# Moving the matmul operands of a two-block transformer kernel onto multiples of 256 bytes in SBUF

## The chip, the cores and the metric

The kernel runs on one core of a Trainium2 chip. The metric is the device time of one execution in microseconds (us). Three executions of the kernel before took 2682.97, 2686.71 and 2687.61 us; the median is 2686.71 us.

## The reference, cut to what matters

The input `x` is 512 tokens of 1024 features, in fp32. It passes two blocks.

```
first_block, for l in (0, 1):
    h = rms_norm(x); proj = h @ w_in            # 1024 -> 10 pieces
    6 heads of difference attention, 6 heads of grouped attention, 4 heads over a memory of 256
    x = x + rms_norm(concat(heads * silu(gates)) @ w_out)
second_block, for i in (0, 1):
    x = x + 0.5 * rmsnorm(swiglu(rmsnorm(x)))   # 1024 -> 2 x 2816 -> 1024
    x = x + rmsnorm(mixer(rmsnorm(x)))          # i = 0: S5 state space; i = 1: gated convolution, 31 taps
    x = x + 0.5 * rmsnorm(swiglu(rmsnorm(x)))
```

All arithmetic keeps about fp32's precision.

## The kernel before, in words

**Three products for one.** Weights and activations are each split into a high part of the type fp32r (fp32 bits, which TensorE takes in one pass) and a low part, the rest. `mm3` (lines 157 to 161) then issues three matmuls into the same PSUM bank: high by high (L159), high by low (L160), low by high (L161). Nearly every matmul of the kernel comes from these three lines. `load` (lines 134 to 155) brings 128 x 1024 weights per DMA, splits them on ScalarE (L148) and on VectorE or GpSimd (L153), and hands them on by pieces.

**The order of the work.** Eight phases run one after the other: attention layer 0, attention layer 1 (`attn`, lines 351 to 785), the first feed-forward block f00, S5 (`s5`, 1026 to 1157), f01, f10, the convolution (`conv`, 1166 to 1280) and f11. Each ends in an output projection (`out_proj`, 261 to 278, or the tail of `ffn`), which adds to `x` and normalizes the tokens for the next phase. The framework works out the order of instructions on each engine and the places of the tiles; tiles that don't live at the same time share places.

**A feed-forward block** (`ffn`, lines 281 to 348) has 22 hidden blocks of 128. Up, per block: 2 halves x 8 slices of 128 features x 3 matmuls of 512 columns, 48 in all; the stationary operand is a weight slice, the moving one (read column by column) is `self.act(k)`, the normalized activations. The first two blocks are done in two halves of 256 columns (192 matmuls). Down: two passes (keys `DN`, h = 0 and 1), in each 22 slices x 4 tokens blocks x 3 matmuls of 512 columns, 264 in all; the stationary operand is a piece of the gated tile `gts[k]`, the moving one is weights. A gated tile comes from one of two tags:

```
if f not in (4, 5) and f < 12:
    gt = self.tl("u4", [P, 2, 512], F32R)
else:
    if f % 2 == 0:
        pair = self.tl("u8", [P, 2, 2, 512], F32R)
    gt = pair[:, f % 2]
```

The down passes go through k = 0 to 21 in order, and there the tag of the stationary operand is the only thing of the operands that changes (in f00, f01 and f10).

**Where tiles lie.** The framework packs tiles by size from the bottom of SBUF, a partition's 229,376 bytes up to its last 32. In the built program of the kernel before the places of the tiles are these (bytes in a partition, and the remainder to 256):

| tiles | first byte | remainder |
|---|---|---|
| `base`: the activations `act0`, `act1` (line 76), `identr`, `wh` | 16,512 | 128 |
| `x`, then the tag `u8` (among them gated tiles of f = 4, 5 and 12 to 21, queries and keys of the attention, `zz` of the convolution) | 50,784 to 116,320 | 96 |
| `const`: `ident`, `fold`, `ones`, `par` | 116,320 | 96 |
| tags `u4`, `raw`, `w`, `wf` (weights) and smaller ones | 121,088 upward | 0 |

Slices inside these tiles that a matmul reads begin at further multiples of 512 bytes, except `zz[:, p, i:i + 512]` in the convolution's taps (line 1229), which begins 4 bytes later at each tap i. In f11, when `base` is no longer needed, some weight tiles of its down passes are put into that memory and so also have the remainder 128.

**Small things that the change touches.** `mh` holds -0.5 in one column; `pow_` (line 181) reads it on GpSimd as the exponent. It is a column of `const`.

Of the kernel before, what the change touches and what calls it, by code (L numbers as in the profile page):

```python
# [8 lines left out]
F32 = mybir.dt.float32  # L9
F32R = mybir.dt.float32r  # L10
# [4 lines left out]
P = 128  # L15
# [50 lines left out]
class Kern:  # L66
    def __init__(self, ctx, tc, aps):
        self.tc, self.nc, self.a = tc, tc.nc, aps
        nc = self.nc
        self.pool = ctx.enter_context(tc.tile_pool(name="sb", bufs=1))  # L70
        self.psp = ctx.enter_context(tc.tile_pool(name="ps", bufs=1, space=bass.MemoryType.PSUM))
        self.dram = ctx.enter_context(tc.tile_pool(name="dr", bufs=1, space=bass.MemoryType.DRAM))
        self.cnt = 0
        base = self.sb([P, 8568], F32R, "base", 1)
        acts = base[:, 0:8192].rearrange("p (a k r c) -> p a k r c", a=2, k=4, r=2)
        self.act0, self.act1 = acts[:, 0], acts[:, 1]
        self.identr = base[:, 8192:8320]
        rest = self.sb([P, 1192], F32, "const", 1)
        self.par = rest[:, 400:1192]
        self.ident, self.fold, self.mh = rest[:, 0:128], rest[:, 128:192], rest[:, 192:193]  # L80
        self.neglam, self.lam, self.mag, self.s5d, self.bgl = rest[:, 194:196], rest[:, 196:200], rest[:, 200:232], rest[:, 232:264], rest[:, 264:272]
        self.ones = rest[:, 272:400]
        self.wh = base[:, 8320:8568].rearrange("p (f e) -> p f e", f=8)
        make_identity(nc, self.ident)
        nc.vector.tensor_copy(self.identr, self.ident)
        nc.gpsimd.memset(self.mh, -0.5)
        nc.vector.tensor_tensor(out=self.fold, in0=self.ident[:, 0:64], in1=self.ident[:, 64:128], op=ALU.add)
        self.flip = self.turn = self.wcnt = 0
        self.on_pool, self.on_dve = (), ()
        self.wt = "w"  # L90
        self.first = 0
# [1370 lines left out]
```

## Time and profile before

| | |
|---|---|
| median of three executions | 2686.71 us |
| the profiled execution, its own time | 2685.91 us |
| its span, first to last instruction | 2684.1 us |
| PE busy (TensorE matmul) | 95% of the span, 13437 records |
| PEld busy (TensorE weight load) | 81% |
| DVE, ACT, POOL busy | 55%, 39%, 25% |
| mean granted TensorE clock | 0.98 |
| moved by DMA | 98 GB/s on the mean |

DVE is VectorE, ACT ScalarE, POOL GpSimd. A matmul's record lasts longer than the distance to the next one's start, because matmuls are pipelined: records overlap. What a matmul costs in a dense stretch is therefore the stretch divided by the number of matmuls that start in it. The profile names every on-chip tile `t`, so operands are told apart by the line and by the order of the loops.

### The profile page before, as it was taken

The page shows a single profiled execution, that of the slowest core. Times are in us where ns is not written, and L with a number is a line of the kernel's source. Part 1 is how long each engine was busy: PE and PEld are TensorE (multiplying, and loading weights), DVE is VectorE, ACT ScalarE, POOL GpSimd, SP SyncE. Part 2 cuts the span into 40 slices and gives each one's busy share as a digit, 9 for nine tenths or more (in the row PEclk, how much of TensorE's full clock was granted, in tenths as well). Part 3 has the DMA queues.
Part 4 walks back from the last instruction along what each step waited for, and adds up shares of the span by engine and source line. Part 5 has one row for each costly group of instructions (what it writes and reads, how often), then busy time and mean ns, then how long its engine had stood idle before and what let it go on. Part 6 is the DMA issues. An engine that isn't in the chain of part 4 may idle for free.

```text
span 2684.1 us, 34384 instructions
## 1 busy us (share of the span) xinstructions
PE 2558.3 (95%) x13437; PEld 2170.8 (81%) x13437; DVE 1471.3 (55%) x2330; ACT 1034.2 (39%) x1961; POOL 666.4 (25%) x880
## 2 busy tenths in 40 slices
PE   7998999989999999989999999999999966999998
PEld 7997889878888888888888888888888844888887
DVE  7788577875589832595533323433324697533322
ACT  4567554675434432323422223322223423322221
POOL 4653245432256600322200001100003940200000
PEclk9999999999999999989999999999999988999999
DMA  4211232112235433352222222322232210222221
GB/s 150 74 63 66 74 115 74 54 53 73 104 118 188 183 135 121 145 209 75 99 94 91 94 102 87 110 94 94 95 108 77 77 54 25 94 94 102 87 95 71
DMA packets 68898, 262.80 MB, mean 98 GB/s; under 512 B 7936, under 2 KB 8448, under 8 KB 64384
## 3 DMA queue, kind: packets, MB, share of 16 engines
q1 hardware_dynamic: 68736, 260.61, 27.5%
q8 instruction: 105, 1.72, 0.3%
q14 instruction: 57, 0.47, 0.1%
HBM read 239.61 MB, written 20.97 MB: 97 GB/s over the span
## 4 chain that ended last, share of the span: by engine, by line
PE 51%; DVE 3%; POOL 1%; ACT 1%; issue 0%; DVEq 0%; POOLq 0%; ACTq 0%
PE t L160 17%; PE t L161 17%; PE t L159 17%; DVE t L1235 2%; POOL t L153 0%; PE t L1244 0%; PE t L214 0%; PE t L1261 0%; DVE t L1242 0%; ACT t L200 0%; ACT t L148 0%; ACT t L232 0%; PE t L1102 0%; DVE t L206 0%; PE t L1103 0%
## 5 line engine op out<-in xcount | busy, mean ns | idle before, releaser
L159 PE MATMUL t<-t,t 128*128 128x512 f32 (+3 forms) x3571 | 1309.5, 369 | 15.2 <-ACT t L166 12.3
L160 PE MATMUL t<-t,t 128*128 128x512 f32 (+3 forms) x3571 | 1308.8, 367 | 6.8 <-DVE t L167 3.3
L161 PE MATMUL t<-t,t 128*128 128x512 f32 (+3 forms) x3571 | 1304.5, 367 | 2.5 <-DVE t L167 2.4
L159 PEld LDWEIGHTS t<-t,t 128*128 128x128 f32 x3571 | 674.4, 189 | 133.8 <-ACT t L166 17.4
L153 DVE TENSOR_TENSOR t<-t,t 128x1024 fp32r<-128x1024 f32 (+2 forms) x314 | 389.8, 1244 | 706.1 <-ACT t L148 510.8
L160 PEld LDWEIGHTS t<-t,t 128*128 128x128 f32 x3571 | 675.7, 189 | 123.1 <-DVE t L167 6.0
L161 PEld LDWEIGHTS t<-t,t 128*128 128x128 f32 x3571 | 675.4, 189 | 115.1 <-DVE t L167 4.2
L148 ACT ACTIVATE t<-t 128x1024 fp32r<-128x1024 f32 (+2 forms) x370 | 384.0, 1045 | 549.4 <-PE t L160 405.9
L235 POOL TENSOR_SCALAR t<-t,t 128x1 f32<-128x1 f32 x32 | 10.7, 335 | 1322.9 <-ACT t L232 1321.6
L166 ACT ACTIVATE t<-t 128x512 fp32r<-128x512 f32 (+3 forms) x316 | 155.6, 517 | 289.2 <-DVE t L297 119.6
L167 DVE TENSOR_TENSOR t<-t,t 128x512 fp32r<-128x512 f32 (+3 forms) x316 | 198.9, 647 | 75.4 <-ACT t L166 75.2
L153 POOL TENSOR_TENSOR t<-t,t 128x512 fp32r<-128x512 f32 (+4 forms) x102 | 191.0, 1889 | 78.8 <-ACT t L148 56.8
L296 ACT ACTIVATE t<-t 128x512 f32<-128x512 f32 x88 | 52.6, 598 | 308.6 <-PE t L161 296.2
L555 ACT ACTIVATE t<-t,t 128x512 f32<-128x512 f32 (+1 forms) x176 | 113.5, 654 | 39.9 <-DVE t L553 37.5
L1235 DVE SCALAR_TENSOR_TENSOR t<-t,t,t 128x512 f32<-128x512 f32 x161 | 116.3, 752 | 10.9 <-PE t L161 7.5
L553 DVE TENSOR_REDUCE t<-t 128x1 f32<-128x512 f32 (+1 forms) x160 | 105.5, 680 | 16.5 <-PE t L563 7.8
L297 DVE TENSOR_TENSOR t<-t,t 128x512 f32<-128x512 f32 x88 | 60.5, 687 | 84.5 <-PE t L161 84.2
L621 DVE TENSOR_TENSOR t<-t,t 128x512 fp32r<-128x512 f32 x112 | 76.0, 685 | 37.7 <-ACT t L616 31.2
L958 POOL TENSOR_TENSOR t<-t,t 128x64 f32<-128x64 f32 (+3 forms) x112 | 65.8, 606 | 70.5 <-DVE t L886 48.7
L976 DVE TENSOR_TENSOR t<-t,t 128x256 f32<-128x256 f32 x128 | 65.5, 575 | 21.7 <-DMA t<-in_s5bc 21.5
L183 POOL TENSOR_TENSOR t<-t,t 128x1 f32<-128x1 f32 (+2 forms) x98 | 74.1, 757 | 6.9
L206 DVE SCALAR_TENSOR_TENSOR t<-t,t,t 128x512 f32<-128x512 f32 x72 | 57.9, 845 | 26.9 <-POOL t L183 26.9
(220 smaller groups left out, 2165.3 us busy)
## 6 DMA issues: line engine op xcount, KB each, us to landing
t<-in_W SPq DMA_DIRECT2D x356, 512.0 KB, 3.5
mats<-t SPq DMA_DIRECT2D x16, 1024.0 KB, 4.1
t<-mats SPq DMA_DIRECT2D x16, 1024.0 KB, 5.4
t<-in_gv SPq DMA_DIRECT2D x19, 512.0 KB, 3.7
t<-in_W SPq DMA_DIRECT2D x24, 384.0 KB, 3.1
t<-in_W SPq DMA_DIRECT2D x8, 480.0 KB, 4.1
t<-in_x SPq DMA_DIRECT2D x4, 512.0 KB, 7.0
t<-in_mem SPq DMA_DIRECT2D x4, 512.0 KB, 6.2
```

The source lines that it names most:

```text
L148: nc.scalar.activation(h[:, :c], raw[:, :c], AF.Copy)
L153: eng.tensor_tensor(out=l[:, o:o + m], in0=raw[:, o:o + m], in1=h[:, o:o + m].bitcast(F32), op=ALU.subtract)
L159: mm(out, lhs[0], rhs[0], start=start, stop=False)
L160: mm(out, lhs[0], rhs[1], start=False, stop=False)
L161: mm(out, lhs[1], rhs[0], start=False, stop=stop)
L166: nc.scalar.activation(h, src, AF.Copy)
L167: nc.vector.tensor_tensor(out=l, in0=src, in1=h.bitcast(F32), op=ALU.subtract)
L183: self.nc.gpsimd.tensor_tensor(out=r, in0=r, in1=self.mh.to_broadcast([P, n]), op=ALU.pow)
L553: v.tensor_reduce(out=mx[:, q * w:q * w + w], in_=part, axis=AX.X, op=ALU.max, negate=True)
L555: act.activation(e[:, i], part[:, i - q * w], AF.Exp, bias=mx[:, i:i + 1], accum_out=u["d"][:, i:i + 1])
L621: v.tensor_tensor(out=lo, in0=tp, in1=h.bitcast(F32), op=ALU.subtract)
L1235: v.scalar_tensor_tensor(out=pc, in0=z[:, i:i + 512], scalar=cp[:, f, 5 + i:6 + i], in1=pc, op0=ALU.mult, op1=ALU.add)
```

## The change

`base` gets 40 more columns of 4 bytes: 32 in front, which shift everything else in it by 128 bytes, and 8 behind. `mh` moves into the first of the columns in front. `const` gets 24 more columns. Together that is 256 bytes more per partition. No instruction is added or taken away. Packed in the same order, `base` then ends at byte 50,944, `const` begins at 116,480 and the rest at 121,344, all multiples of 256; the activations begin at 16,640, which is one too. `zz` is read at the same 4-byte steps as before.

```
-        base = self.sb([P, 8568], F32R, "base", 1)
+
+        base = self.sb([P, 8608], F32R, "base", 1)
+        self.mh = base[:, 0:1].bitcast(F32)
+        base = base[:, 32:8608]
         acts = base[:, 0:8192].rearrange("p (a k r c) -> p a k r c", a=2, k=4, r=2)
         self.act0, self.act1 = acts[:, 0], acts[:, 1]
         self.identr = base[:, 8192:8320]
-        rest = self.sb([P, 1192], F32, "const", 1)
+        rest = self.sb([P, 1216], F32, "const", 1)
         self.par = rest[:, 400:1192]
-        self.ident, self.fold, self.mh = rest[:, 0:128], rest[:, 128:192], rest[:, 192:193]
+        self.ident, self.fold = rest[:, 0:128], rest[:, 128:192]
```

## Rows read from the trace of the kernel before

**Rows 1.** The page, part 1: busy time, share of the span, instructions.
```profile
PE 2558.3 (95%) x13437; PEld 2170.8 (81%) x13437; DVE 1471.3 (55%) x2330; ACT 1034.2 (39%) x1961; POOL 666.4 (25%) x880
```

**Rows 2.** Busy time by stretch: length; PE, PEld, DVE, ACT, POOL; clock; DMA.
```profile
0.00:303.00 303.00, 274.27 (x1919) 256.37 (x1919) 227.72 (x445) 186.18 (x449) 140.80 (x207) 0.99 0.25 84
303.00:368.00 65.00, 64.23 (x326) 54.24 (x325) 39.58 (x53) 25.58 (x56) 16.98 (x23) 1.00 0.37 130
368.00:648.00 280.00, 260.65 (x1852) 243.67 (x1851) 217.10 (x395) 173.77 (x422) 126.76 (x182) 0.98 0.19 63
...
697.00:1098.00 401.00, 396.60 (x1895) 329.78 (x1896) 252.67 (x565) 144.00 (x255) 133.75 (x227) 0.99 0.39 140
1098.00:1302.00 204.00, 191.35 (x1190) 171.40 (x1190) 143.13 (x158) 71.12 (x139) 57.97 (x57) 0.95 0.37 136
1302.00:1690.00 388.00, 384.21 (x1801) 316.13 (x1800) 137.38 (x149) 116.19 (x165) 28.80 (x35) 1.00 0.28 98
1690.00:2054.00 364.00, 363.33 (x1633) 296.12 (x1631) 120.50 (x130) 103.70 (x139) 10.95 (x16) 1.00 0.27 94
2054.00:2302.00 248.00, 201.70 (x906) 159.16 (x907) 188.36 (x276) 91.55 (x165) 120.43 (x100) 0.90 0.15 54
2302.00:2685.00 383.00, 373.36 (x1702) 304.52 (x1700) 125.78 (x139) 102.44 (x138) 14.35 (x21) 0.99 0.27 94
```

**Rows 3.** PE by stretch, f10's first down pass: k 0-3, 4-5, 6-11, 12-21.
```profile
1929.73:1940.63 10.90, 10.90 (x49) 1.00 0.34 122
1940.63:1946.24 5.61, 5.61 (x25) 1.00 0.35 137
1946.24:1962.59 16.35, 16.35 (x73) 1.00 0.29 97
1962.59:1990.70 28.11, 28.11 (x121) 1.00 0.28 94
```

**Rows 4.** The same: f10's up blocks 2-21; f11's first down pass, k 6-9, 10-11.
```profile
1705.73:1929.73 224.00, 224.00 (x962) 1.00 0.27 94
...
2571.01:2581.92 10.91, 10.91 (x50) 1.00 0.04 15
2581.92:2587.51 5.59, 5.59 (x26) 1.00 0.01 3
```

**Rows 5.** PE in order of time (start, length, line): tap 4, two convolution blocks.
```profile
2097.16 0.39 PE L159 MATMUL t<-t,t 128*128 128x512 f32 x1
2097.38 0.40 PE L160 MATMUL t<-t,t 128*128 128x512 f32 x1
2097.62 0.40 PE L161 MATMUL t<-t,t 128*128 128x512 f32 x1
```

**Rows 6.** The same tap, the convolution's next block of 128 features.
```profile
2111.80 0.39 PE L159 MATMUL t<-t,t 128*128 128x512 f32 x1
2112.02 0.40 PE L160 MATMUL t<-t,t 128*128 128x512 f32 x1
2112.26 0.40 PE L161 MATMUL t<-t,t 128*128 128x512 f32 x1
```

**Rows 7.** PE by stretch, matmuls of one width: 384, 320, 256 columns.
```profile
354.75:360.03 5.28, 5.28 (x32) 1.00 0.88 300
438.29:442.56 4.27, 4.27 (x31) 1.00 0.25 77
1694.94:1705.62 10.68, 10.68 (x92) 1.00 0.27 98
```

**Rows 8.** Waits of PE, 0 to 303 us: us in total, times, longest.
```profile
PE t L214 <- DVE t L206: 11.7, 3, 7.8
```

**Rows 9.** Waits of PE in the convolution, 2054 to 2303 us.
```profile
PE t L1244 <- DVE t L1242: 42.0, 5, 10.0
```

**Rows 10.** The page, parts 5 and 6: the split on ScalarE; the weights' DMAs.
```profile
L148 ACT ACTIVATE t<-t 128x1024 fp32r<-128x1024 f32 (+2 forms) x370 | 384.0, 1045 | 549.4 <-PE t L160 405.9
...
t<-in_W SPq DMA_DIRECT2D x356, 512.0 KB, 3.5
```

## The prediction

> **What bounds the kernel now.** I read the page's busy shares first. PE is busy 95% of the span and no other engine more than 55% apart from its own weight loads [rows 1]. A share over the whole span hides that stages differ, so I cut the span into the phases [rows 2]. There the reader should look for stretches where PE busy equals the length. In the four feed-forward blocks (697 to 1098, 1302 to 1690, 1690 to 2054, 2302 to 2685) PE is busy 1517.5 of 1536 us, at a granted clock of 0.99 to 1.00; DVE is at a third to two thirds and the DMA engines at 0.27 to 0.39 of their time. The first attention layer's output projection (303 to 368) looks the same. In these stretches the time is the number of matmuls times the distance between their starts, and nothing else. The attention's middles (0 to 303 and 368 to 648) have PE busy 534.9 of 583 us; there PE waits for VectorE and ScalarE, the longest sum being for L206, three waits with 11.7 us, 7.8 the longest [rows 8]. The convolution is PE-free for a fifth of its time, and one wait, L1244 for VectorE's L1242, makes up 42.0 us of that [rows 9].
>
> So the question is whether the distance between matmuls depends on where their operands begin. The trace before answers it in one place, because the down passes change the place of the stationary tile in mid-loop and nothing else. In f10 [rows 3] the record counts include one matmul that began before the stretch, so the counts by the loops are 48, 24, 72 and 120. That makes 10.90 / 48 = 227.1 ns for k = 0 to 3, 5.61 / 24 = 233.8 ns for k = 4, 5, then 16.35 / 72 = 227.1 ns, then 28.11 / 120 = 234.3 ns. The quick ones are just those k whose gated tile has the remainder 0, with weights of remainder 0; the slow ones have 96. In f11 k = 6 to 9 take 10.91 / 48 = 227.3 ns, but k = 10, 11, whose gated tiles are still at remainder 0, take 5.59 / 24 = 232.9 ns: there the weights have moved into memory with remainder 128 [rows 4]. The up blocks, moving operand at 128, take 224.00 / 960 = 233.3 ns [rows 4]. One operand off is enough, and a second off costs no more.
>
> **The change, part by part.** The first part is what it does to a matmul of 512 columns: 233.3 - 227.1 = 6.2 ns saved in an up block, 7.0 ns (234.1 on the mean of the slow down rows) in a down pass, 6.5 ns where I have no row of its own (the projections, scores, gates of S5).
>
> The second part is narrower matmuls. No quick row exists for them. The slow rows are 5.28 / 30 = 176 ns for 384 columns, 4.27 / 29 = 147 ns for 320 and 10.68 / 90 = 118.7 ns for 256 [rows 7]. If the loss grows with the columns, a 256-column matmul saves 3.3 ns (half of 6.6); if it is one price per matmul, 6.6 ns. The nearest row doesn't decide, so I take the middle: 5.0 ns for 256, 5.3 for 320, 5.8 for 384, and keep both ends. Nothing excludes that they gain nothing, which the wide range below includes.
>
> The sum, at the profiled execution's 2685.9 us (its span of 2684.1 and 1.8 around it):
> - Feed-forward, PE-bound, so all of it counts. Up: 4 x 960 x 6.2 ns = 23.8 us. First two blocks in halves: 4 x 192 x 5.0 = 3.8 us. Down: 528 matmuls a block, of which 240 are quick already; 288 x 7.0 = 2.0 us in each of f00, f01, f10. In f11, 408 are slow, but some 256 of them read weights in the memory that `base` leaves; that memory still begins at 16,512, remainder 128, so I leave them slow: 152 x 7.0 = 1.1 us. Together 35 us.
> - Attention's output projections, dense in rows 2: 2 x 192 x 6.5 = 2.5 us.
> - Attention's middles. 576 matmuls of 384 columns (3.3 us), 384 of 320 (2.0), 1472 of 256 (gates, memory queries, values, memory scores: 7.4), 288 of 512 (scores, memory projection: 1.9): 14.6 us if PE alone sets the pace, 0 if VectorE and ScalarE do. PE is busy 92% here and VectorE 76% (227.7 + 217.1 of 583 us) [rows 2], so both set the pace by turns; I take half, 7.3 us.
> - S5: its glu and output projection, 2 x 192 x 6.5 = 2.5 us; its input projection 384 x 5.0 = 1.9 us, half of it because it alternates with the scan: 3.5 us.
> - Convolution. The first double projection runs ahead of VectorE: 192 x 5.0 = 1.0 us; the output projection 192 x 6.5 = 1.3 us. The other projections (288 x 6.6 = 1.9 us) run while PE is waiting for VectorE anyway; I cost them at nothing, because that wait of 42.0 us covers it. The taps stay at their 4-byte steps: nothing. Together 2.3 us.
> - The fp32 transposes and the few fp32 products with `ident`, `fold`, `ones`: some 1,700 records of about 110 ns. Bounded by 0 and by the same 2.9%, 5 us; I take 0, since the only quick rows are fp32r.
> - The move of `mh`: GpSimd's powers read another column; no instruction and no wait is added, and writes into other columns of `base` already run beside reads of it, as the dense up blocks after each normalization show. I cost it at nothing; if each power waited half a microsecond, all but those at the ends of phases would still fall beside PE's work.
>
> 35 + 2.5 + 7.3 + 3.5 + 2.3 = 50.6 us, so 2685.9 - 50.6 = 2635.3 us for the profiled execution. The median of the runs stands 0.8 us above that one: 2636 us.
>
> What is late next: in the feed-forward blocks nothing comes near. Per up block PE will need 21.8 us instead of 22.4, and the DMA share would rise from 0.27 to 0.28 [rows 2]. In the attention the waits for VectorE grow; that is the half I left out.
>
> A page bears on the size. The Trainium skill, "TensorE: Matmul & The Clock Gate", section "Wait — 56ns, not 53.3ns?", gives 215.7 ns for 512 columns back to back on a warm array. By that figure, as an estimate from the page, aligned matmuls would save 17.6 ns and not 6.2, and the up blocks alone 68 us. The rows at remainder 0 stand at 227.1 [rows 3], so the trace disagrees and I go by it.
>
> **The rivals.**
> *No change: the place isn't what makes the down rows differ.* In the map, remainder 0 goes together with high memory (from 121,088 up), remainders 96 and 128 with low memory. If TensorE reads high memory quicker, or if only steps smaller than these tiles' remainders matter, nothing gains: 2686 us, within a microsecond. For it: rows 3 and 4 can't tell place from remainder. Against it: the taps. Their two moving operands lie in one low tile, 2,168 bytes apart, and at tap 4 the high part's matmul takes 2097.38 - 2097.16 = 0.22 us and the low part's 0.24 us; in the next block, whose tile lies 4,352 bytes (17 x 256) further, again 0.22 and 0.24 us [rows 5, 6]. The low bits of the address matter inside one region.
> By the Trainium skill, "SBUF — State Buffer", section "Door 1: The DMA port swizzle", SBUF has lines of 16 bytes and only the crossing to a new line costs. Both 96 and 128 are multiples of 16, so by that rule this rival would hold. The steps in rows 3 are not explained by it.
>
> *Partly: only the up blocks or only the stationary operand gain.* After the change the activations lie at an odd multiple of 256 and the weights, 256 bytes further up, at an even one; all quick rows of now have both at odd multiples. If part of the pairs stay slow, between a quarter and two thirds of the sum come: 2653 to 2674 us, say 2660.
>
> *Slower: the new packing makes PE wait for weights in the attention.* SBUF is full to the last 32 bytes, and 256 more are asked for; the packer must hand some places on in another order, and a tile that takes over a place waits for its last reader. The place is the loads of the attention's chunks: 24 of them (12 per layer). One that starts late exposes at least the DMA's landing and the first split, 3.5 and 1.0 us [rows 10]. At 24 x 3 us = 72 us against the gain of 51 us the time is 2707 us; it decides from 2.1 us per chunk. For it: the number of buffers a tag may use is fixed, but not the places. Against it: the tile sizes grow only in the two tiles that live throughout, and PE has few long waits in the attention [rows 8], with the DMA at 0.19 to 0.25.
>
> **How the numbers follow.** The forecast has 0.72, its own range 2613 to 2647. The quick end counts every sum whole (50.6 + 7.3 + 1.0 + 1.9 = 60.8 us, 2626), and takes off 5.5 us for narrow matmuls at 6.6 ns, 5 for fp32 and 1.7 for f11's weights. The slow end counts only feed-forward, with 3.3 ns for narrow matmuls (33.4 us), and the dense projections (6.3 us). Partly has 0.13, no change 0.10, slower 0.05. The range for 8 in 10 is 2609 to 2663: the forecast and the nearer half of the partial case. A change below 0.2%, 5.4 us, can't be told from none here. Faster: 0.72 + 0.13 = 0.85, same 0.10, slower 0.05.
>
> **What would show it.** In the profile after, the up blocks of f10 should take 20 x 48 x 227 ns = 217.9 us where they took 224.0, and the down passes 227 ns from k = 0 to 21 without a step. A 256-column stretch shows whether the narrow price is 3.3 or 6.6. The taps' 0.22 and 0.24 should remain. The granted clock and the wait L1244 for L1242 should stay, the latter perhaps a little longer. The prediction is wrong if up blocks stay at 233 ns (place, not remainder), if they gain and the attention's stretches grow (packing), or if the clock falls below 0.98.

## The result, and the profile after

The changed kernel takes 2656.24 us (median of four executions, 2653.88 to 2657.20) against 2687.03 us before. The ratio is 0.9887 with a 95% interval of 0.9870 to 0.9904. The forecast was 2636 us. The direction holds and so does the wide range (2609 to 2663), but the gain is 30.8 us and not 51, and the time lies outside the range that the forecast itself had (2613 to 2647), inside that of the rival "partly" (2653 to 2674).

The page of the kernel after, part 1, answers to [rows 1]: PE's share is still 95%, with 33 us less of it; the other engines do the same work in nearly the same time.

```profile
PE 2525.2 (95%) x13437; PEld 2175.8 (82%) x13437; DVE 1472.7 (55%) x2330; ACT 1032.8 (39%) x1961; POOL 666.0 (25%) x880
```

Next the dense stretches of f10 after the change, PE by stretch, in the order of rows 4 and 3: the up blocks 2 to 21, then the first down pass with k = 0-3, 4-5, 6-11, 12-21; the last two are f11's k = 6-9 and 10-11.

```profile
1692.07:1909.70 217.63, 217.63 (x963) 1.00 0.28 97
1909.70:1920.58 10.88, 10.88 (x50) 1.00 0.33 119
1920.58:1926.02 5.44, 5.44 (x26) 1.00 0.41 147
1926.02:1942.34 16.32, 16.32 (x74) 1.00 0.27 97
1942.34:1969.54 27.20, 27.20 (x122) 1.00 0.28 97
...
2543.36:2554.24 10.88, 10.88 (x50) 1.00 0.28 96
2554.24:2559.68 5.44, 5.44 (x26) 1.00 0.30 97
```

The up blocks take 217.63 / 960 = 226.7 ns a matmul where they took 233.3 [rows 4]. The down pass has lost its step: 10.88 / 48, 5.44 / 24, 16.32 / 72 and 27.20 / 120 are all 226.7 ns, where k = 4, 5 and 12 to 21 stood at 234 [rows 3]. In f11, k = 10, 11 came down too: in the built program of the kernel after none of that block's weights lie where `base` was any more. Those of k = 10, 11 lie among the other weights, and 64 of the block's matmuls read theirs where `const` was, all at remainder 0.

The narrow matmuls are another matter. These are the stretches that answer to [rows 7]: 384, 320 and 256 columns.

```profile
356.09:361.30 5.21, 5.21 (x31) 1.00 0.91 314
439.60:443.85 4.25, 4.25 (x31) 1.00 0.25 77
1681.16:1691.95 10.79, 10.79 (x91) 1.00 0.27 97
```

384 columns went from 176 to 5.21 / 30 = 173.7 ns, 320 from 147.2 to 146.6, and 256 from 118.7 up to 10.79 / 90 = 119.9 ns.

By phase (the columns of rows 2; the stretches are cut at the phases of the kernel after):

```profile
0.00:304.40 304.40, 275.49 (x1911) 257.28 (x1912) 227.98 (x445) 185.76 (x448) 139.79 (x206) 0.98 0.25 83
...
368.00:647.00 279.00, 260.76 (x1857) 243.31 (x1856) 218.09 (x398) 173.35 (x421) 126.36 (x182) 0.99 0.19 63
...
696.00:1091.00 395.00, 389.52 (x1895) 329.38 (x1896) 254.14 (x565) 143.39 (x255) 133.60 (x227) 0.99 0.39 142
1091.00:1295.00 204.00, 190.37 (x1195) 172.57 (x1193) 142.98 (x158) 70.73 (x139) 58.30 (x57) 0.95 0.38 137
1295.00:1675.00 380.00, 375.35 (x1786) 315.94 (x1785) 137.27 (x149) 115.92 (x164) 29.09 (x34) 1.00 0.29 100
1675.00:2032.00 357.00, 356.07 (x1643) 297.27 (x1641) 121.14 (x130) 104.31 (x142) 11.08 (x16) 1.00 0.27 96
2032.00:2280.00 248.00, 201.59 (x909) 160.95 (x909) 188.46 (x276) 91.48 (x165) 120.39 (x100) 0.89 0.16 54
2280.00:2654.00 374.00, 364.88 (x1697) 305.65 (x1696) 125.40 (x139) 102.24 (x138) 14.10 (x20) 0.99 0.27 96
```

The four feed-forward blocks shrank (401 to 395, 388 to 380, 364 to 357, 383 to 374 us against [rows 2]). The attention's middles (303 and 280 us before), S5 (204) and the convolution (248) did not. The convolution's wait kept its size, as the prediction said of it [rows 9]:

```profile
PE t L1247 <- DVE t L1245: 42.2, 5, 10.0
```

Both kernels issue the same 13437 matmul records in the same order, so the distance from each to the next can be compared one by one between the two traces. I call a pair dense when the clock is full in both and neither distance is over 1.35 times the usual one for its width. Summed over the pairs, before to after: dense 512 columns -41.1 us, 256 columns +2.1, 384 -0.6, 320 -0.1, fp32 and transposes +0.2; pairs at half clock in one of the traces +5.4; pairs with a wait +3.7. The sum is -30.4 us, the difference of the two spans (2684.1 and 2653.8).

### The profile page after: what moved, and what is told of

The parts are those of the page before. It is cut to its first block, busy times and chain, and to the rows that moved or that the text cites. A ratio compares the mean times of both kernels' runs of the same rounds, so it can differ in the third digit from the quotient of the medians.

```text
span 2653.8 us, 34395 instructions
## 1 busy us (share of the span) xinstructions
PE 2525.2 (95%) x13437; PEld 2175.8 (82%) x13437; DVE 1472.7 (55%) x2330; ACT 1032.8 (39%) x1961; POOL 666.0 (25%) x880
## 4 chain that ended last, share of the span: by engine, by line
PE 51%; DVE 3%; ACT 1%; issue 0%; POOL 0%; DVEq 0%; POOLq 0%; ACTq 0%
PE t L163 16%; PE t L162 16%; PE t L164 16%; DVE t L1238 2%; PE t L217 0%; PE t L1264 0%; DVE t L241 0%; PE t L1247 0%; ACT t L203 0%; ACT t L235 0%; DVE t L1245 0%; DVE t L209 0%; DVE t L170 0%; ACT t L151 0%; PE t L1105 0%
```

## The experiments

**Is it the remainder, and in which tiles?** Three kernels move other tiles, or move them by other amounts; a fourth measures matmuls by themselves.

The probe, in short:

```
for n, m, s in CASES:            # columns, remainder of moving, remainder of stationary
    for i in range(48):
        matmul(ps[:, 0:n], buf[s + slice i % 32], buf[m + slice i % 8], start=(i == 0), stop=(i == 47))
```

> This kernel leaves out the whole transformer: it copies x into one fp32r tile and runs 35 groups of 48 dense fp32r matmuls, all operands in that one low tile, each group with its own columns (512 to 256), its own remainder to 256 bytes of the moving operand and of the stationary one. Its whole time says nothing; the distance between matmuls in each group does. Theory (remainder): 512 columns with both at 0 take 227 ns; any group with one or both operands off takes 232 to 236; 256, 320 and 384 columns take the same on and off (119.6, 146.5, 174.7 ns in the kernel after), and 448 or 480 show where the loss begins. Rival (region): all operands lie in one low tile, so all 512-column groups take the same, 233 ns if low memory is what is slow. Rival (16-byte lines, the Trainium skill, page SBUF - State Buffer, section Door 1): only the groups at remainder 4 and 8 are slow, all multiples of 16 take the same.

PE by stretch, from the first start to the last of a group, 47 distances each, written as (columns, remainder of the moving operand, of the stationary one): (512, 128, 0), (512, 0, 128), (512, 128, 128), (512, 96, 96), (512, 64, 0), then 256 columns at (0, 0) and (128, 0).

```profile
98.75:109.72 10.97, 10.97 (x49) 1.00 0.00 0
177.12:188.05 10.93, 10.93 (x48) 1.00 0.01 1
199.29:209.97 10.68, 10.68 (x49) 1.00 0.00 0
210.20:220.88 10.68, 10.68 (x49) 1.00 0.01 2
76.54:87.31 10.77, 10.77 (x49) 1.00 0.00 0
339.06:344.69 5.63, 5.63 (x49) 1.00 0.00 0
344.81:350.39 5.58, 5.58 (x49) 1.00 0.00 0
```

One operand off gives 233.4 and 232.6 ns, as in the kernel. But both off by the same gives 10.68 / 47 = 227.2 ns, the quick distance, at 128 and at 96 (and at 64). So my theory fell here: it is not the remainder of an operand, but the two operands' remainders against each other. In pairs of remainders at 512 columns, (64, 0) stands at 229.1, (0, 64) at 233.3, (192, 0) at 233.3 and (0, 192) at 228.9: the groups order by moving minus stationary, modulo 256. The region is no part of it, since quick and slow groups lie in one low tile. And 16-byte lines don't tell the groups apart: at a moving remainder of 16, 32, 96, 128 or 192 the mean is 231.6 to 233.6. At 256 columns the difference 128 is even a little quicker (118.7) than 0 (119.8). At the widths between, the loss shrinks unevenly, both at 0 against (128, 0): 216.6 and 220.1 ns at 480 columns, 202.8 and 203.9 at 448, 173.4 and 176.1 at 384, 146.5 and 146.6 at 320.

```
-        base = self.sb([P, 8568], F32R, "base", 1)
+        base = self.sb([P, 8632], F32R, "base", 1)
+        base = base[:, 32:8632]
```

> Only the activations (and identr, wh) are moved to remainder 0; queries, keys, gated tiles of the tag u8 and const stay at 96, mh stays in const. 512-column matmuls with both operands at 0 rise from about 850 to 5736. Theory (remainder, 512 columns alone gain): 4890 x 6.3 ns = 31 us of PE time less, of which waits, the clock and 2000 narrow matmuls at 0.8 ns more give back about a quarter: 2661 us (2656 to 2666), up blocks at 227 ns, slow pieces of the down passes still at 234. Rival (the new order of places or the moved mh makes the gain, not the remainder): no more than a third of the 31 us, 2676 us or above.

2663.72 us, ratio 0.9919 (0.9905 to 0.9934), as the theory expected. Dense 512-column pairs are 29.3 us shorter than before; 8 us of it is given back, in part at half clock (3.7) and in waits (3.1). The up blocks run at 217.63 / 960 = 226.7 ns, and in the down pass k = 4, 5 stay slow (the stretches are up, k = 0-3, k = 4-5):

```profile
1697.41:1915.04 217.63, 217.63 (x962) 1.00 0.30 97
1915.04:1925.92 10.88, 10.88 (x49) 1.00 0.40 120
1925.92:1931.54 5.62, 5.62 (x26) 1.00 0.42 141
```

```
-        base = self.sb([P, 8568], F32R, "base", 1)
+        base = self.sb([P, 8608], F32R, "base", 1)
-        rest = self.sb([P, 1192], F32, "const", 1)
+        rest = self.sb([P, 1216], F32, "const", 1)
```

> The counterpart: activations stay at remainder 128, everything else that begins at 96 moves to 0, mh stays in const. 512-column matmuls with both at 0 rise from about 850 to 2352. Theory: 1500 x 7 ns = 10.5 us of PE time less, net 2679 us (2676 to 2682), down passes without a step at 227 ns, up blocks at 233. The two kernels' gains in dense stretches add up to the change's 41 us. Rival (packing or mh): no relation to these counts.

2679.38 us, ratio 0.9980 (0.9970 to 0.9991), as the theory expected. The mirror image: the up blocks keep 224.00 / 960 = 233.3 ns, k = 4, 5 are quick. Dense 512-column pairs are 9.5 us shorter.

```profile
1701.78:1925.78 224.00, 224.00 (x962) 1.00 0.29 94
1925.78:1936.68 10.90, 10.90 (x50) 1.00 0.40 120
1936.68:1942.12 5.44, 5.44 (x26) 1.00 0.41 146
```

29.3 + 9.5 = 38.8 us against the whole change's 41.1; most of the rest is f11's weights, which only the whole change puts at an equal remainder. `mh` stays in `const` in both kernels, so its move has no part in this. Packing as the cause is out: each half gains where its own operands now agree. Both kernels put these operands at remainder 0, so they can't tell "at 0" from "equal"; the next one can.

```
-        base = self.sb([P, 8568], F32R, "base", 1)
+        base = self.sb([P, 8576], F32R, "base", 1)
-        rest = self.sb([P, 1192], F32, "const", 1)
+        rest = self.sb([P, 1216], F32, "const", 1)
```

> Every tile that holds matmul operands is put to remainder 128, those at 0 in the kernel before too. Theory: the 850 matmuls that are quick in the kernel before lose 6.6 ns each, 5.6 us: 2692 us (2689 to 2695), and no 512-column stretch at 227 ns is left. Rival (only a difference between the two operands' remainders costs, as in the kernel before at 128 against 0 or 0 against 96): with both operands at 128 all become quick, as in the kernel after, 2656 us.

2654.15 us, ratio 0.9884 (0.9869 to 0.9899): as quick as the change itself, with no operand at a multiple of 256. The theory expected 2692, its rival 2656. The stretches are up, k = 0-3 and 4-5, all at 226.7 ns:

```profile
1690.45:1908.08 217.63, 217.63 (x963) 1.00 0.30 97
1908.08:1918.96 10.88, 10.88 (x50) 1.00 0.39 118
1918.96:1924.40 5.44, 5.44 (x26) 1.00 0.43 150
```

**Which differences are quick?** The second probe goes through all 64 differences.

> Leaves out the whole transformer: 118 groups of 24 dense fp32r matmuls in one low tile. 512 columns with the stationary operand at remainder 0 and the moving one at 0, 4, ... 252; four groups in which the odd matmuls' operands are moved by 128, so that a matmul's moving operand has the remainder of its own stationary operand, or that of the next one's; 256 columns in steps of 8; 384 in steps of 16. Theory (difference: the read of the moving operand meets the load of the next stationary one): 227 ns at difference 0, 229 at 64, 232 to 236 at 96, 128, 192 and 4; the group whose moving operand agrees with the next stationary one is quick, that which agrees with its own alone is slow. Rival (equal remainders of a matmul's own two operands): the other way round. For 256 and 384 columns both say nothing; from the first probe 118.6 to 119.9 and 173.4 to 176 ns. If another difference is quicker than 0, the kernel can gain from it.

The stretches are, 23 distances each: 512 columns at difference 20, at 192 and at 0; the group with a matmul's own operands equal and the next stationary one 128 off; the group with the next one equal and its own off; 256 columns at difference 0 and at 192.

```profile
48.98:54.49 5.51, 5.51 (x24) 1.00 0.00 0
290.42:295.78 5.36, 5.36 (x24) 1.00 0.00 0
380.32:385.54 5.22, 5.22 (x24) 1.00 0.00 0
385.77:391.03 5.26, 5.26 (x24) 1.00 0.00 0
391.26:396.55 5.29, 5.29 (x24) 1.00 0.00 0
407.88:410.63 2.75, 2.75 (x25) 1.00 0.00 0
476.45:479.08 2.63, 2.63 (x26) 1.00 0.00 0
```

At 512 columns the difference 0 is the quickest of the 64, 5.22 / 23 = 227 ns; the others have 229 to 240, most of those four bytes past a multiple of 16 being among the worst (239.6 at 20). The two mixed groups shown have 228.7 and 230.0 ns, both between quick and slow (the other two, in which one operand alone alternates, 232.5 and 230.0), so neither the theory nor its rival on which stationary operand is met came out: that stays open. Nor does the difference alone fix the last 3 ns: (0, 4) and (252, 0) have the same one and take 232.4 ns in the first probe and 230.0 here, (0, 16) and (240, 0) take 233.3 and 236.1. At 256 columns the best is not 0 (2.75 / 23 = 119.6) but 192 (2.63 / 23 = 114.3).

**Can narrow matmuls gain with their own difference?** The changed kernel once more, beside two that begin some weights later inside their tile:

```
+    def shift(self, key):
+        return 16 if key[0] in ("U", "CI") and key[-1] < 2 else 0
-            h = self.tl(self.wt, [P, 1024], F32R)
-            l = self.tl(self.wt, [P, 1024], F32R)
+            sh = self.shift(key)
+            h, l = (self.tl(self.wt, [P, 1088 if sh else 1024], F32R)[:, sh:sh + 1024] for _ in range(2))
```

> The changed kernel once more, beside the two that follow, on the same chip: 2654 to 2657 us. Theory (the time at half clock scatters from run to run): its granted clock lies between 0.979 and 0.982 and the runs order by it. Rival (the change itself costs clock): all runs at 0.979 to 0.980, below those of the kernel before at 0.980 to 0.983.

2655.25 us, ratio 0.9887 (0.9871 to 0.9903); granted clocks 0.978 to 0.980, nearer to the rival.

> The changed kernel, with the weights of the first two up blocks of each feed-forward block and of the first two projections of the convolution begun 64 bytes later, so that 960 matmuls of 256 columns have the difference moving minus stationary 192 (all 512-column ones keep 0). Theory (difference, as in the second probe: 114.0 ns at 192, 119.9 at 0): 960 x 5.9 = 5.7 us less, dense and bound by PE: 2651 us (2649 to 2653). Rival (the probe's 114 holds only for its own order of slices): 2656 us, 256-column stretches still at 119.6 ns.

2653.49 us, ratio 0.9875 (0.9861 to 0.9889), whose interval overlaps that of the changed kernel beside it: neither the theory's time nor the rival's slow matmuls. The matmuls did what the probe said: f10's first two blocks, 90 distances, stand first for the changed kernel's second run, then for this one (where the columns of all five engines follow the length).

```profile
1680.12:1690.92 10.80, 10.80 (x92) 1.00 0.30 97
```

```profile
1679.44:1689.66 10.22, 10.22 (x92) 10.22 (x91) 4.68 (x6) 4.91 (x7) 0.00 (x0) 1.00 0.17 51
```

10.22 / 90 = 113.6 ns against 120.0. Pair by pair, the dense 256-column distances of the two traces are 4.8 us shorter, but the span only 3.3 and the medians 1.8. The four feed-forward blocks together went only from 1493.1 to 1490.2 us. These matmuls stand at the head of a phase, where PE waits for the normalized tokens: the waits for ScalarE's split there, summed over the run, went from 14.0 to 16.0 us.

```profile
PE t L162 <- ACT t L169: 14.0, 14, 3.0
```

```profile
PE t L165 <- ACT t L172: 16.0, 13, 3.0
```

```
+        if key[0] in ("GT", "MQ", "SI"):
+            return 48
...
-    per = 1024 // n
+    per = 3 if key and key[0] in ("GT", "MQ", "SI") else 1024 // n
```

> Besides, the weights of the attention's gates and memory queries and of S5's input projection begin 192 bytes later (moving 192, stationary 0) and are loaded in groups of three slices instead of four: 1344 more matmuls of 256 columns at 114 ns, 7.9 us of PE time. Theory (PE sets half the pace there): 2647 us (2644 to 2650). Rival (VectorE and ScalarE set the pace, or the smaller groups of weights come later): 2651 us or more, with the PE time saved turned into waits.

2640.97 us, ratio 0.9829 (0.9815 to 0.9843), the quickest kernel here and better than the theory's 2647. That was a reason for distrust, so the last run keeps the smaller groups and takes the 48 columns away again:

> The last kernel but with the weights of gates, memory queries and S5's input projection at remainder 0 again; only their smaller groups (three slices per load) stay. Theory (remainder: the last kernel's gain beyond the first two up blocks, some 12 us, is the 1344 matmuls at 114 to 115 ns): 2650 to 2653 us, those stretches back at 119.6 ns. Rival (the smaller groups let weights arrive earlier and the remainder adds little): 2641 to 2644 us. Between the two both take part.

2643.19 us, ratio 0.9838 (0.9825 to 0.9851). The rival is right: most of that gain, some 10 of 12 us, is the smaller groups of weights. The 1344 matmuls do become quicker in the profiled executions (115.6 instead of 119.6 ns where dense, 5 us together), but by the medians that adds only some 2 us, and the two intervals overlap. The gain of the smaller groups shows in the attention, whose two layers go from 697.6 us in the changed kernel's second run to 691.7, and most in S5. PE, PEld, DVE, ACT, POOL, clock and DMA over that phase, for the changed kernel's second run and for this one:

```profile
1090.20:1296.60 206.40, 190.33 (x1194) 172.40 (x1192) 144.10 (x160) 73.41 (x145) 60.35 (x60) 0.95 0.38 134
```

```profile
1085.40:1282.70 197.30, 185.57 (x1193) 166.81 (x1191) 142.26 (x163) 73.96 (x149) 59.31 (x59) 0.99 0.40 143
```

9.1 us less at a mean clock of 0.99 instead of 0.95. Several pauses of PE of 1 to 3.7 us, in the input projection and ahead of the glu's last slices, are gone there, and with them most of the half-clock time. Whether the earlier pieces or the other order of work did it was not tried. The smaller groups also mean 382 splits on ScalarE instead of 370, and they change by count which of VectorE and GpSimd makes the low part of a piece.

## Why the prediction was right or wrong, point by point

- **Where the time is bound.** Right for the feed-forward blocks: PE-bound nearly without gaps, they gave 29 us of the 30, of 35 forecast. For the rest it was too hopeful. From the first matmul of a phase to that of the next, the attention gave 1.1 us of 9.8 forecast, the convolution 0.1 of 2.3, and S5 became 0.2 us longer where 3.5 were forecast. Their dense 512-column pairs did become 6.8 us shorter together; waits, half clock and the narrow matmuls took nearly all of it back.
- **The size for 512 columns.** Right but for a tenth: 6.2 ns in an up block and 7.0 in a down pass were forecast, 6.6 and 7.1 to 7.6 came. The sum had 38 us of these; the pairs show 41.1, with f11's weights (1.7 us, left slow in the sum) and the convolution's projections (1.9, costed at nothing) in it.
- **The reason.** Wrong, though it gave the right number. The step was "One operand off is enough, and a second off costs no more." The kernel before has no dense 512-column stretch whose two operands are off by the same amount, so its rows could not show that the second cancels the first. (Its 96 score matmuls of L563 have queries and keys both at 96, but they stand singly or by twos between matmuls of other lines.) That the size held all the same is luck: the change puts both operands at 0, where the wrong rule and the right one forecast the same. The rival that counted the two operands' relation was priced only as a partial gain; the case in which nothing need be at a multiple of 256 was not among the rivals.
- **Narrow matmuls.** This is the term that failed most. "I take the middle: 5.0 ns for 256, 5.3 for 320, 5.8 for 384" put 12 us into the sum (3.8 in feed-forward, 6.4 in the attention, 1.0 and 1.0 in S5 and the convolution); measured they gave +1.4 us. The nearest rows were all slow ones, and a line through slow rows says nothing about a quick one. The prediction named a gain of nothing as possible and still took the middle. The probe shows why nothing came: at 256 columns the differences 0 and 128 are alike (119.8 and 118.7 ns).
- **Half of the attention's saving.** Too much as well. Making the narrow ones quick after all brought by the medians 2 us of 5.7 at the phases' heads and 2 of 7.9 in the attention and S5, each within overlapping intervals.
- **Waits and clock.** Costed at nothing; the traces show +3.7 us in pairs with waits and +5.4 at half clock. The waits that grew most are those for ScalarE's split of the normalized tokens (12.3 to 14.0 us) and for GpSimd's L1090 in S5 (2.7 to 3.5); why was not tried. The clock is not settled. By the prediction's own sign ("if the clock falls below 0.98") the change fails here, with 0.979 in the profiled execution. Of 28 runs of the kernel before, 27 have 0.980 to 0.983 and one 0.978; the eight of the change have 0.978 to 0.980, which is nearly what the rival of the repeated run expects; but the kernel with everything at 128, with the same distances between its matmuls, has 0.979 to 0.981.
- **The slower rival** (packing makes PE wait for weights) did not come: the order of PE's matmuls is the same and its longest waits are the same ones, as the wait that answers to [rows 8] shows (0 to 304 us):

```profile
PE t L217 <- DVE t L209: 11.6, 3, 7.9
```

- **Partly.** The measured 2656 us lies in this rival's range, but not by its mechanism: up blocks and down passes all gained, to 226.7 ns. What was missing stood elsewhere, in the narrow matmuls, the waits and the clock.
- **No change**, the rival of regions and of 16-byte lines, is out by the first probe. The prediction's own argument against it, the taps, was weaker than it reads. L161 reads the same high part as L159, at the same remainder and with a stationary operand of the same remainder, and takes 0.24 us [rows 5] to the next start:

```profile
2097.86 0.39 PE L159 MATMUL t<-t,t 128*128 128x512 f32 x1
```

So 0.22 and 0.24 can't be told from what the neighbouring matmuls do. As the prediction said, the taps, whose operands keep their difference, stayed: at the same tap after the change, to a rounding,

```profile
2076.25 0.39 PE L162 MATMUL t<-t,t 128*128 128x512 f32 x1
2076.48 0.40 PE L163 MATMUL t<-t,t 128*128 128x512 f32 x1
2076.72 0.40 PE L164 MATMUL t<-t,t 128*128 128x512 f32 x1
2076.95 0.39 PE L162 MATMUL t<-t,t 128*128 128x512 f32 x1
```

## What to carry to other kernels

Where a loop's rate steps with nothing but an operand's place, compare the places of both operands of the matmul and not each with a round number: here, at 512 columns, equal remainders were enough, whether at 0 or at 128. Take a price only from rows of the same width; where there are none, count nothing for it and keep the rest as a bound (here nothing was what came). A saving on matmuls that stand at the head of a phase or between other engines' work was worth little here; don't count it before the trace shows those stretches dense.

## What the runs showed of the hardware that was not expected

The distance of dense fp32r matmuls, each with its own stationary operand, goes with the moving operand's start minus the stationary one's, modulo 256 bytes: at 512 columns 227 ns at 0, 229 at 64, 231 to 236 at the other multiples of 16, up to 240 between them; at 256 columns 120 at 0, 114 at 192, with much the same values in the probe and in the kernel (113.6 in f10). It is the rule of uniform streams. Where the differences alternate, the neighbours count too (the mixed groups, the taps). The Trainium skill, "SBUF — State Buffer", section "Who interferes with whom", gives PE two independent read ports, one for the moving operand and one for the weights, and says that PE never waits on anyone. These runs go against "independent" in so far as the places of PE's two operands against each other change its pace (227 against 233 ns); whether it is the two reads that meet, and how, no run here shows.
